# Last set of the retention's output projection by ordinary products, layer 2's input split over two sets, another form of the keys' norm, and retention tiles laid out anew

## The chip, the cores and the metric

The kernel runs on one core of a Trainium2 chip. A core has five engines with queues of their own, which meet only at semaphores: TensorE (PE, with its weight loads shown apart as PEld), VectorE (DVE), ScalarE (ACT), GpSimd (POOL) and SyncE (SP, which here only issues DMAs). Each queue runs in order: an instruction that waits holds all that stand behind it. The metric is the device time of one launch in microseconds (us), lower is better.

## The reference

One inference step of a two-layer decoder trunk over 1024 prompt tokens and 8 sample tokens, model width 1024, all in float32. Layer 1 is a retention, layer 2 attention in a sliding window:

```python
def retention_layer(x, S0, g_norm, w_in, g_out, w_out):      # 4 heads, DK 256, DV 512, chunks of 128
    h = rmsnorm(x, g_norm)
    q, k, v, gate = jnp.split(h @ w_in, [RET_QK, 2 * RET_QK, 2 * RET_QK + RET_V], axis=-1)
    k = k * (RET_DK ** -0.5)
    # chunk by chunk: o = (q k^T * decay) v + decay' * q S ;  S = S * decay'' + (k * decay''')^T v
    o, S = retention_scan(q, k, v, S0)
    o = rmsnorm(o, g_out) * jax.nn.silu(gate)                # 1024 x 2048
    return x + o @ w_out, S                                  # w_out is 2048 x 1024

def swa_layer(x, g_norm, w_in, q_gain, k_gain, sinks, w_out, ...):   # 16 heads, 2 key heads of 64
    h = rmsnorm(x, g_norm)
    q, k, v, gate = jnp.split(h @ w_in, [SWA_Q, SWA_Q + SWA_KV, SWA_Q + 2 * SWA_KV], axis=-1)
    q = rmsnorm(q, q_gain); k = rmsnorm(k, k_gain)           # per head of 64
    o = banded_attention(q, k, v, sinks) * jax.nn.silu(gate)
    return x + o @ w_out, k, v
```

The two row norms matter here. With x the row of layer 2's input (already times the gain), r = (mean(x^2) + EPS)^-0.5 and y = x @ w_k, a key is (r y) * (mean((r y)^2) + EPS)^-0.5 times its gain. Since r is one number per row, the same value is y * (mean(y^2) + EPS * (mean(x^2) + EPS))^-0.5.

## The kernel before, in words

A float32 operand of a product is split in a high half (rounded by ACT) and a low half (what is left, by a subtraction on DVE or POOL), and a product is three matmuls: high by high, low by high, high by low.

**Retention.** After the input projection (up to about 541 us) come 32 steps, one for each head and chunk, to about 684 us. A step (lines L778 to L1089) reads evp, evx and evc or evw, which SP loads from scratch tensors in DRAM, transposes them, makes S (the state's update) and po (the output) on PE, and on the side vh, vl, Sh, Sl (halves of the values and the state), the statistics ss and the normed output `on`, which PE transposes into `tr` at L104. All these tiles are cut out of one pool by `lay` in a written order, over the space of tiles that older work used; a tile must wait for the last reader of what lay there. The first two steps read operands that lie elsewhere (`first` in the profile). `x_decode` is a generator that loads the sample rows' input (memset on POOL, four DMAs on SP at L1117, transposes on DVE) in three parts, at steps of the table `others`.

**Output projection.** `psets` holds eight sets. Set n computes for half P = n // 4 of the inner width the quarter a = n % 4 of the output columns, 256 of them. A plain set has 8 slots of 24 matmuls (`p_plain`, L1301): 4 groups of tokens (keys c, w, x, p) by 2 halves t. The other kind has 14 slots of 12 matmuls (`p_prod`, L334 to L336): seven products of sums of quarters in the manner of Strassen and Winograd, for which POOL and DVE form the sums (`p_sum`: S1 to S4), ACT and DVE or POOL the halves (`p_hi`, `p_lo` at L1174), and for which the products are put together from PSUM banks that several results share (`p_evac`, L1196 to L1206). Sets 0 to 3 are plain and leave partial results in DRAM (`p_store`), which the sets 4 to 7 load (`p_part`) and add. `p_fins` then finishes a group of tokens: the gain and halves into SA, layer 2's input (L1251 on ACT, L1261 on DVE), its sum of squares `acc` (L1263), the columns for the sample rows, and a store of the residual.

SA also holds the operands B and T of the sets themselves, in cells that `CELL` numbers. So layer 2's input cannot be written in place where a cell is still read: the columns of sets 4 to 6 are stored to DRAM (`xscr`), loaded again (`a_load(k)`, 512 KB, k = 0 to 5, on SP) and split there (`a_split(k, 0)` on ACT, `a_split(k, 1)` on DVE at L1393); those of set 7 are written directly.

Between the slots of PE, the orders of ACT, DVE, POOL and SP are written by `later(slot, ...)` and `when(time, ...)`: the instruction goes into its engine's queue at that slot of PE's order.

**Layer 2's keys and values.** Nine chunks c = 0 to 8 (the last is the 8 sample rows). `kv_mm(c, h)` makes half h of a chunk's 24 matmuls (L1757 to L1759) into a bank that is `pj` or `sc` by turns. `rstd9` sums acc on PE and makes r9 and e9 = EPS * (mean + EPS) for four or five chunks; `kv_ev(c)` makes the values vv (ACT) and the normed key kd (ACT squares `kj`, DVE `kss`, POOL `krk`, DVE L1739); `kv_tr` transposes kd, and `kv_kk` splits it. Two chunks' first halves run ahead of the loop. Between them ACT and POOL convert weights for the next stage (`wh`, `wl`), and `rbcast_mm` spreads r9 into `rbc`. From about 908 us projections of q and gate run with the attention, whose order the scheduler of the language makes, and then the output projection.

## Time and profile before

| | us |
|---|---|
| median of 3 runs | 1314.88 (1314.08 to 1314.96) |
| the profiled execution | 1315.55 |
| its span, first to last instruction | 1313.6 |
| input projection, from the start to about | 541 |
| 32 steps of the retention, to about | 684 |
| sets 0 to 3, plain, to | 777.8 |
| sets 4 to 7, by seven products, to | 864.3 |
| keys and values, to | 908.4 |
| projections, attention, output, to the end | 1313.6 |

A row of a timeline gives start and duration in us, engine, line, operation and tiles, and in brackets how long the engine had been idle and what released it. Of the kinds of rows, the waits (engine and line that waited, what released it, us in total, times, longest) tell where an engine stood still; a table of windows gives for each stretch the busy time of each engine with its count of instructions, the clock that TensorE was granted, the busy share of the DMA engines and GB/s. A clock below 1.00 means that matmuls came at longer intervals in part of the window.

### The profile page before, as it was taken

The numbers are of one execution on the slowest core, as the hardware profiler recorded it, in microseconds if no ns is written. First come the engines' busy times: TensorE is split into PE (matmuls) and PEld (weight loads), VectorE is DVE, ScalarE is ACT, GpSimd is POOL, SyncE is SP. The second block draws the span as 40 slices with busy tenths as digits, with TensorE's granted clock in tenths as the row PEclk, the third lists the DMA queues.
The fourth block names the chain that finished last, engine by engine and source line by source line (L and its number), as shares of the span: only waits on it lengthen the run. The fifth ranks groups of instructions, "written<-read, shape, count | busy, mean of one in ns | idle before, by whom it ended". The sixth has DMA issues, their size and how long they took to land.

```text
span 1313.6 us, 26814 instructions
## 1 busy us (share of the span) xinstructions
PE 1271.3 (97%) x9815; PEld 1217.2 (93%) x9815; DVE 764.5 (58%) x1475; ACT 668.7 (51%) x1656; POOL 754.3 (57%) x903
## 2 busy tenths in 40 slices
PE   6999999999999999899999999978999999999998
PEld 6999999999999999888889999968998999998998
DVE  6944556565566674477763755653665666766321
ACT  5533544554555553578761343445576676666121
POOL 6654544545458898789661658626476676554000
PEclk9999999999999999999999999999998999999999
DMA  6314767677676754556879856732032211237232
GB/s 225 104 60 129 239 197 243 182 234 220 197 221 188 231 179 121 173 170 205 270 208 280 210 178 173 209 88 85 17 98 81 65 57 42 77 108 252 73 96 77
DMA packets 220911, 205.62 MB, mean 157 GB/s; under 512 B 32697, under 2 KB 195765, under 8 KB 220765
## 3 DMA queue, kind: packets, MB, share of 16 engines
q1 hardware_dynamic: 188784, 169.56, 43.1%
q10 hardware_dynamic: 31996, 34.36, 8.2%
q8 instruction: 77, 1.26, 0.4%
q14 instruction: 54, 0.43, 0.1%
HBM read 134.36 MB, written 70.55 MB: 156 GB/s over the span
## 4 chain that ended last, share of the span: by engine, by line
PE 84%; POOL 5%; DVE 3%; ACT 3%; issue 2%; DMA 2%; SPq 0%; ACTq 0%; POOLq 0%; DVEq 0%
PE S L1301 7%; PE b L334 7%; PE b L336 7%; PE b L335 7%; PE pj L1654 6%; PE pj L1655 6%; PE pj L1656 6%; PE b L327 4%; PE tr L104 4%; PE b L328 4%; PE b L329 4%; PE o L2017 2%; PE b L543 2%; PE sc L1980 1%; PE S L336 1%
## 5 line engine op out<-in xcount | busy, mean ns | idle before, releaser
L334 PE MATMUL b<-xh,woh 128*128 128x258 f32 x784 | 223.2, 285 | 0.0
L336 PE MATMUL b<-xh,wol 128*128 128x258 f32 x784 | 221.9, 283 | 1.3 <-POOL wol L225 1.3
L335 PE MATMUL b<-xl,woh 128*128 128x258 f32 x784 | 221.6, 283 | 0.0
L1654 PE MATMUL pj<-SA,wh 128*128 128x384 f32 (+1 forms) x512 | 174.8, 341 | 2.1 <-ACT SA L2037 1.3
L1655 PE MATMUL pj<-SA,wh 128*128 128x384 f32 (+1 forms) x512 | 164.7, 322 | 0.2 <-DVE SA L2038 0.2
L1656 PE MATMUL pj<-SA,wl 128*128 128x384 f32 (+1 forms) x512 | 164.8, 322 | 0.0
L334 PEld LDWEIGHTS b<-xh,woh 128*128 128x128 f32 x784 | 148.0, 189 | 4.1 <-issue 4.1
L336 PEld LDWEIGHTS b<-xh,wol 128*128 128x128 f32 x784 | 148.0, 189 | 1.7 <-POOL wol L225 1.7
L335 PEld LDWEIGHTS b<-xl,woh 128*128 128x128 f32 x784 | 148.7, 190 | 0.0
L225 POOL TENSOR_TENSOR wol<-raw,woh 128x512 fp32r<-128x512 f32 x52 | 68.1, 1319 | 119.7 <-ACT woh L220 108.6
L327 PE MATMUL b<-woh,xh 128*128 128x256 f32 x448 | 126.6, 283 | 0.0
L328 PE MATMUL b<-wol,xh 128*128 128x256 f32 x448 | 126.0, 281 | 0.0
L329 PE MATMUL b<-woh,xl 128*128 128x256 f32 x448 | 125.6, 280 | 0.0
L1654 PEld LDWEIGHTS pj<-SA,wh 128*128 128x128 f32 x512 | 97.0, 190 | 5.9 <-issue 2.6
L1655 PEld LDWEIGHTS pj<-SA,wh 128*128 128x128 f32 x512 | 97.3, 190 | 0.4 <-DVE SA L2038 0.4
L1656 PEld LDWEIGHTS pj<-SA,wl 128*128 128x128 f32 x512 | 96.7, 189 | 0.0
L1995 POOL TENSOR_TENSOR s<-s,sm 128x512 f32<-128x512 f32 x64 | 66.6, 1040 | 47.9 <-DVE sm L1994 43.7
L327 PEld LDWEIGHTS b<-woh,xh 128*128 128x128 f32 x448 | 84.3, 188 | 5.0 <-issue 2.9
L220 ACT ACTIVATE woh<-s 128x512 fp32r<-128x512 f32 x88 | 54.1, 624 | 59.7 <-POOL s L210 22.0
L329 PEld LDWEIGHTS b<-woh,xl 128*128 128x128 f32 x448 | 84.3, 188 | 0.0
L328 PEld LDWEIGHTS b<-wol,xh 128*128 128x128 f32 x448 | 84.3, 188 | 0.0
L1987 ACT ACTIVATE s<-s,mx 128x257 f32<-128x257 f32 x128 | 64.2, 505 | 36.1 <-DVE mx L1985 35.3
(521 smaller groups left out, 3650.4 us busy)
## 6 DMA issues: line engine op xcount, KB each, us to landing
raw<-in_w_in_ret_dram ACTq DMA_DIRECT2D x44, 512.0 KB
st<-in_state_ret_dram SPq DMA_DIRECT2D x64, 256.0 KB
out_dram<-st SPq DMA_DIRECT2D x64, 256.0 KB
vb<-vscr SPq DMA_DIRECT2D x64, 128.0 KB
evp<-qks SPq DMA_DIRECT2D x32, 256.0 KB
evx<-vsc SPq DMA_DIRECT2D x32, 256.0 KB
wr<-in_w_in_swa_dram SPq DMA_DIRECT2D x32, 256.0 KB
evc<-gsc SPq DMA_DIRECT2D x16, 256.0 KB
```

Of the source, the lines that this page charges most:

```text
L225: eng.tensor_tensor(lo, src_of(s, name, sub), hi.bitcast(F32), SUB)
L327: mm(dst, xh, wh, start=a and i == 0, stop=False, skip_group_check=True)
L328: mm(dst, xh, wl, start=False, stop=False, skip_group_check=True)
L329: mm(dst, xl, wh, start=False, stop=z, skip_group_check=True)
L334: mm(dst, wh, xh, start=a, stop=False, **sg)
L335: mm(dst, wh, xl, start=False, stop=False, **sg)
L336: mm(dst, wl, xh, start=False, stop=z, **sg)
L1301: mm(box[0], s.op[f"A{i + 1}{j + 1}", 0][w][:, k, :], xs_[t][x[j]][:, k, :], start=(xs_ is XH and w == 0 and j + k == 0), stop=(xs_ is XL ...
L1654: mm(ps, hi[:, k, fs], xh[:, k, t0:t1], start=first and k == ks[0], stop=False)
L1655: mm(ps, hi[:, k, fs], xl[:, k, t0:t1], start=False, stop=False)
L1656: mm(ps, lo[:, k, fs], xh[:, k, t0:t1], start=False, stop=last and k == ks[-1])
L1995: nc.gpsimd.tensor_tensor(st[:, :, 0:256], st[:, :, 0:256], sm.unsqueeze(2).broadcast_to([128, 2, 256]), ALU.mult)
```

## The change

Seven things are done at once.

1. Set 7 becomes a plain set: 192 matmuls in place of 168, without S1 to S4, with four operands instead of seven to split, and with its own banks for every result. `p_part` loads all four partial tiles of it into ring tiles, and `p_plain`, for a set with P = 1, finishes each group of tokens by `p_fins` after slot 3 of the set at the earliest.
2. In the sets that are not plain, the low half of A22 goes from POOL to DVE (`p_lo`).
3. The cells of B and T are numbered anew, so that cells 0 to 3 hold T2 and T1. `a_load` of k = 0 to 3 goes to slots 4 to 7 of set 6 (v is its first slot, u that of set 7), with splits at v+9, v+12, u and u+2; k = 4 and 5 are loaded at u+4 and split at u+5 and u+6.
4. Set 7 reads T3 as its plain operand: it is loaded again from DRAM at slots v+10 and v+11 and split at u and u+1. So that it is still there, the sums that were stored over it go to a scratch of their own, `tsc`.
5. `knorm_a` adds e9 in place of EPS and takes the squares without the scale r; the product of krk with r falls away; vv stands behind the squares in ACT's order. Both forms give the same key, as shown above.
6. No first half of a chunk runs ahead: `kv_mm(n, 0)` stands right in front of `kv_mm(n, 1)` and what belongs between them.
7. `x_decode` has its parts at steps 2, 5 and 9 in place of 3 and 6; the tiles of the retention lie in another order, with a smaller pad.

The first place is SP's order in the retention, where the sample rows' input is loaded (`ra`). Before:

```order
L734 DMA evp<-qks 128x512 x2
L741 DMA evx<-vsc 128x512
L747 DMA evc<-gsc 128x512
L734 DMA evp<-qks 128x512
L741 DMA evx<-vsc 128x512
L747 DMA evw<-gsc 128x512
L1117 DMA ra<-in_x_sample_dram 8x4x64 x4
```

After:

```order
L742 DMA evx<-vsc 128x512
L748 DMA evc<-gsc 128x512
L735 DMA evp<-qks 128x512
L742 DMA evx<-vsc 128x512
L748 DMA evw<-gsc 128x512
L1119 DMA ra<-in_x_sample_dram 8x4x64 x4
```

The four DMAs stand two steps' loads (six rows) later; the step's own three loads follow behind them in both.

The second place is DVE's order in set 7 of the output projection. L1393 is `a_split`, L1261 and L1263 finish columns, L1203 and L1200 empty banks of the seven products. Before:

```order
L1200 TENSOR_TENSOR evx<-b_11089,evp 128x258
L1393 SCALAR_TENSOR_TENSOR SA<-SA,gcol 128x1024
L1200 TENSOR_TENSOR evx<-b_11106,evp 128x258
L1393 SCALAR_TENSOR_TENSOR SA<-SA,gcol 128x1024
L1174 TENSOR_TENSOR w_9196<-s2b,w_9196 128x512
L1203 TENSOR_TENSOR evc<-S,evc 128x258
L1393 SCALAR_TENSOR_TENSOR SA<-SA,gcol 128x1024
L1261 SCALAR_TENSOR_TENSOR SA<-evc,gcol,SA 128x2x128
L1203 TENSOR_TENSOR evc<-S,evc 128x258
L1393 SCALAR_TENSOR_TENSOR SA<-SA,gcol 128x1024
L1261 SCALAR_TENSOR_TENSOR SA<-evc,gcol,SA 128x2x128
```

After, where L1308 empties a bank of a plain set and L1341 splits T3:

```order
L1308 TENSOR_TENSOR evc<-S,evc 128x258
L1341 TENSOR_TENSOR SB<-SB 128x2x256
L1396 SCALAR_TENSOR_TENSOR SA<-SA,gcol 128x1024
L1308 TENSOR_TENSOR evc<-S,evc 128x258
L1341 TENSOR_TENSOR SB<-SB 128x2x256
L1308 TENSOR_TENSOR evp<-S,evp 128x258
L1396 SCALAR_TENSOR_TENSOR SA<-SA,gcol 128x1024
L1308 TENSOR_TENSOR evp<-S,evp 128x258
L1262 SCALAR_TENSOR_TENSOR SA<-evc,gcol,SA 128x2x128 x2
L1264 TENSOR_TENSOR acc<-acc,tr 128x4x128
```

Six splits stood in set 7; four are left there, and two stand among the bank emptyings of set 6.

The third place is ACT's order where the keys and values begin: vv (L1764, then L1770), the squares kj (L1730, then L1737), the weights wh and the spread r9, rbc. Before:

```order
L1764 ACTIVATE vv<-pj,r_78 128x128
L1730 ACTIVATE kj,kss<-pj,r_78 128x64 x2
L1626 ACTIVATE wh<-wr 128x512
L1822 ACTIVATE rbc<-pm 128x384
L1764 ACTIVATE vv<-sc,r_78 128x128
```

After:

```order
L1737 ACTIVATE kj,kss<-pj 128x64 x2
L1770 ACTIVATE vv<-pj,r_79 128x128
L1633 ACTIVATE wh<-wr 128x512
L1827 ACTIVATE rbc<-pm 128x384
L1737 ACTIVATE kj,kss<-sc 128x64 x2
```

The squares come first and read no r; wh and rbc of the first chunks stand where they stood, ahead of chunk 1.

The diff, cut to its core:

```diff
-    for n_, x_ in enumerate((B11, T2, T1, B21, T3, B22, T4)):
+    for n_, x_ in enumerate((T2, T1, B11, B21, T3, B22, T4)):
...
-    lay("Sh1", "Sl1", "sT0", "sTh0", "sTl0", "on0", "qh0", "ql0", "kh0", "kl0", "sT1", "ss0", "ss1", "vl0",
-        "on1", "vh1", "vl1", "kh1", "kl1", "pad", "Sh0", "Sl0", "vh0", "qh1", "ql1", "sTh1", "sTl1")
+    lay("Sh1", "Sl1", "sT0", "sTh0", "sTl0", "qh0", "ql0", "kh0", "kl0", "ss0", "ss1", "sT1", "on1", "kh1", "kl1",
+        "pad", "on0", "vh0", "vl0", "sTh1", "sTl1", "qh1", "Sh0", "Sl0", "vh1", "vl1", "ql1")
...
-        s.n, s.P, s.a, s.kind, s.fw, s.plain = n, n // 4, n % 4, "p", 128, n < 4
+        s.n, s.P, s.a, s.kind, s.fw, s.plain = n, n // 4, n % 4, "p", 128, n < 4 or n == 7
...
-        eng = eng or (pool if name in ("A12", "A22") else dve)
+        eng = eng or (pool if name == "A12" or (name == "A22" and s.plain) else dve)
...
-        if key in "cw":
+        if key in "cw" or s.plain:
             t = c_tile(s, key)
...
-        if t:
+        if s.P:
+            p_fins(s, key, t, max(n, s.n0 + 3))
+        elif t:
             later(n + 2, p_store, s, key)
...
-            nc.sync.dma_start(out=osc[0, 1, t][:, ks], in_=z)
+            nc.sync.dma_start(out=tsc[t][:, ks], in_=z)
...
-        for k in range(6):
-            later(u + 1 + k, a_load, k)
-            later(u + 4 + k, a_split, k, 0)
-            later(u + 5 + k, a_split, k, 1)
+        for t in range(2):
+            later(v + 10 + t, o_load, raw_of(T3, t)[:, :, 0:256], 0, 1, t)
+            split(u + t, T3, t)
+        DC(u + 1, T3, True)
+        for k, (a, b) in enumerate(((v + 4, v + 9), (v + 5, v + 12), (v + 6, u), (v + 7, u + 2), (u + 4, u + 5), (u + 4, u + 6))):
+            later(a, a_load, k)
+            later(b, a_split, k, 0)
+            later(b + 1, a_split, k, 1)
...
-        if i in (3, 6):
-            next(xdg)
+        if i in (2, 5, 9):
+            next(xdg, None)
...
-            nc.scalar.activation(kj[:n], src[:, g * 64:g * 64 + 64], AF.Square, scale=r, accum_out=ss[:n, g:g + 1])
-        nc.vector.tensor_scalar(ss[:n], ss[:n], 1.0 / HD, EPS, ALU.mult, ALU.add)
+            nc.scalar.activation(kj[:n], src[:, g * 64:g * 64 + 64], AF.Square, accum_out=ss[:n, g:g + 1])
+        nc.vector.tensor_scalar(ss[:n], ss[:n], 1.0 / HD, e, ALU.mult, ALU.add)
...
-        nc.gpsimd.tensor_scalar(rk[:n], rk[:n], r, None, ALU.mult)
...
-        nc.scalar.activation(vv[:, c, :], ps[:, 128:256], AF.Copy, scale=r)
-        rk = knorm_a(ps[:, 0:128], r, 128)
+        rk = knorm_a(ps[:, 0:128], e9[:, c:c + 1], 128)
+        nc.scalar.activation(vv[:, c, :], ps[:, 128:256], AF.Copy, scale=r9[:, c:c + 1])
...
-    kv_mm(0, 0)
-    kv_mm(1, 0)
     for n in range(9):
-        if n < 7:
-            kv_mm(n + 2, 0)
+        kv_mm(n, 0)
```

## The prediction

> **What bounds the kernel now.** I read the page first, then the list of what TensorE waited for, then tables of windows, and last the rows around each wait.

> ```profile
> span 1313.6 us, 26814 instructions
> PE 1271.3 (97%) x9815; PEld 1217.2 (93%) x9815; DVE 764.5 (58%) x1475; ACT 668.7 (51%) x1656; POOL 754.3 (57%) x903
> PE 84%; POOL 5%; DVE 3%; ACT 3%; issue 2%; DMA 2%; SPq 0%; ACTq 0%; POOLq 0%; DVEq 0%
> PE pj L1757 <- DVE kd L1739: 3.3, 1, 3.3
> PE S L334 <- DVE evw L1203: 2.4, 2, 2.3
> PE pj L1757 <- DVE evx L1203: 2.3, 1, 2.3
> PE sc L1757 <- ACT wh L1626: 2.3, 1, 2.3
> PE S L336 <- POOL w L1174: 2.0, 2, 1.3
> PE pj L1654 <- ACT wh L1626: 0.8, 1, 0.8
> PE sc L1757 <- DVE evp L1203: 0.6, 1, 0.6
> PE tr L104 <- DVE kkl L1784: 0.6, 1, 0.6
> ```

> TensorE (PE) is busy 97% of the span and carries 84% of the chain that ended last. So another engine's work costs something only where PE stands still for it, and a removed matmul is worth its issue interval. In the list (us, times, longest) the waits at L334 and L336 belong to the output projection of the retention, those at L1757 to the keys and values of layer 2. The windows of these stages (busy us of PE, PEld, DVE, ACT, POOL; clock; DMA share; GB/s) say where PE stands:

> ```profile
> 820.00:841.00 21.00, 21.00 (x177) 21.00 (x176) 13.71 (x24) 9.17 (x21) 17.65 (x13) 1.00 0.59 163
> 841.00:864.30 23.30, 20.88 (x170) 20.29 (x168) 19.04 (x25) 13.52 (x22) 10.02 (x6) 1.00 0.57 180
> 864.30:884.00 19.70, 13.48 (x101) 13.06 (x100) 8.03 (x27) 4.85 (x14) 3.77 (x6) 0.91 0.40 112
> 884.00:908.40 24.40, 20.50 (x146) 18.91 (x146) 8.68 (x33) 13.68 (x51) 14.64 (x21) 0.93 0.16 45
> ```

> Set 6 (first row) leaves PE no gap; set 7 leaves 2.4 us; the stage of keys and values (last two rows, 44.1 us) leaves 44.1 - 13.48 - 20.50 = 10.1 us, and its clock is below 1. That stage is the largest pocket of idle TensorE that the edits touch.

> **The change, part by part.**

> *Start of the retention.* The tiles Sl0, vh0 and vl0 lie elsewhere.

> ```profile
> 543.73 0.39 PE L1022 MATMUL po<-first 128*128 128x512 f32 x1
> 547.13 0.66 PE L104 MATMUL tr<-ident,on 128*128 128x128 f32 x4 [3.01 <-DVE on L1066]
> 544.22 1.29 DVE L1048 SCALAR_TENSOR_TENSOR Sl<-S,Sh 128x512 fp32r<-128x512 f32 x2 [5.28 <-PE po L1022]
> 544.16 0.63 ACT L810 ACTIVATE vh<-evx 128x512 fp32r<-128x512 f32 x1 [1.66 <-PE po L1022]
> ```

> The second step's last matmul (543.73) is what both DVE's Sl (L1048, idle 5.28 before it) and ACT's vh (idle 1.66) wait for, since these tiles lie on operands of that step. Behind Sl in DVE's order stands `on`, for which PE then waits 3.01. In the new layout the vector engine's wait on that matmul is gone: Sl needs only ACT's Sh, and vh waits for no matmul. `on` still needs po, some statistics on ACT and POOL's power; I leave 0.3 of the 3.01 and take **-2.7** (bounds -3.0 and -1.5: the first if all of the wait goes, the second if only ACT's 1.66 goes).

> *Sample row's load.* Its memset goes from step 3 to 2, its four DMAs from 3 to 5, its transposes from 6 to 9.

> ```profile
> 558.89 3.01 SPq L1117 DMA_DIRECT2D ra<-in_x_sample_dram  x4
> 566.02 0.63 ACT L810 ACTIVATE vh<-evx 128x512 fp32r<-128x512 f32 x1 [2.84 <-DMA evx<-vsc]
> 567.63 0.68 PE L778 MATMUL tr<-evp 128*128 128x128 f32 x4 [1.51 <-issue]
> ```

> SP's queue stood before these DMAs for POOL's memset, then took 3.01 us to issue them; evx behind them came late, ACT waited 2.84 and PE 1.51. Two steps later SP meets a finished memset. The 3.01 us of issue stay and push the loads of one step; without the wait for the memset I expect the steps' lead to cover them: **-1.5** (bounds -1.5 and 0: the stall may only move two steps).

> *A22's low half from POOL to DVE in sets 4 to 6.*

> ```profile
> 796.83 0.39 PE L336 MATMUL S<-SB,w 128*128 128x258 f32 x1 [1.31 <-POOL w L1174]
> 793.79 1.74 POOL L1206 TENSOR_TENSOR evx<-evx,rx 128x516 f32<-128x516 f32 x1
> 795.49 1.28 POOL L1174 TENSOR_TENSOR w<-ra,w 128x512 fp32r<-128x512 f32 x1
> 851.50 1.79 DVE L1174 TENSOR_TENSOR w<-s2b,w 128x512 fp32r<-128x512 f32 x1
> ```

> PE waits for a subtraction that stands on POOL behind a 1.74 us sum and takes 1.28 itself. The 2.0 us of the list are two such waits, in sets 4 and 5; set 6 has none. The same line on DVE has taken 1.79 at its longest (last row), and DVE, busy 13.7 of 21 us, reaches it earlier. I take **-2.0** (bounds -2.2, with the slower first matmul after each stall, and -0.7, if only the shorter wait goes).

> *Set 7 by ordinary products.* 192 matmuls in place of 168.

> ```profile
> L1301 PE MATMUL S<-SA,EO x48: 277/282/368, 684.5 to 690.6; 128*128 128x258 f32 x48
> L1301 PE MATMUL S<-SB,w x288: 278/283/290, 719.8 to 777.7; 128*128 128x258 f32 x144
> 860.75 0.36 PE L334 MATMUL S<-SB,w 128*128 128x258 f32 x1 [2.25 <-DVE evw L1203]
> 858.17 1.50 DVE L1261 SCALAR_TENSOR_TENSOR SA<-evc,gcol,SA 128x256 fp32r<-128x256 f32 x1
> 856.18 2.07 DVE L1393 SCALAR_TENSOR_TENSOR SA<-SA,gcol 128x1024 fp32r<-128x1024 f32 x1
> 860.53 1.27 DVE L1393 SCALAR_TENSOR_TENSOR SA<-SA,gcol 128x1024 fp32r<-128x1024 f32 x1
> ```

> The 32 slots of sets 0 to 3 (these rows are the first and last group) run from 684.5 to 777.8 with 0.7 us of transposes between: 92.6 / 32 = 2.9 us a slot. Set 7 becomes 8 x 2.9 = 23.2 us, against 23.3 now: the 24 added matmuls (2.9) eat the removed waits (2.4) and their ramps. The 2.25 us wait goes because DVE no longer runs six splits (L1393) and the chain over one shared bank in the same slots: I count 4 splits x 1.27, 8 evacuations x 0.42, 8 x 0.5 and 4 x 0.7 of finishing and four of 0.7, 18 of 23.2 us, with the evacuations spread over all 8 slots. POOL loses its sums. **-0.1** (bounds -2.4, if tails of the old set are longer than I see, and +2.9, if a DVE stall of the same size comes back).

> *Input split over two sets.* Four of the six 512 KB loads, two of the splits and two reloads of T3 (512 KB each) go to set 6 or its end. That hides under PE's 21 us if DVE and the DMA engines keep up: DVE 13.7 + at most 1.8 (A22) + 2 splits of 1.27 to 2.07 = at most 19.6 of 21; DMA 163 + 3.1 MB / 21 us = 311 GB/s, while the present set 7 moved this while it loaded the same columns:

> ```profile
> 846.00:851.00 5.00, 5.00 (x43) 5.00 (x43) 3.65 (x7) 2.82 (x3) 0.79 (x2) 1.00 0.93 326
> ```

> So set 6 is filled nearly to what one stretch has shown; the leads are 4 to 9 slots of 1.43 us. I cost it at **0**; without cover it is the third rival. The split's own duration is 1.27 at 860.53, when POOL is idle, and 2.07 at 856.18, when POOL runs. [...]

> *Keys and values.* Three edits act together.

> ```profile
> 866.60 0.55 PE L1757 MATMUL pj<-kv,SA 128*128 128x256 f32 x1 [2.29 <-DVE evx L1203]
> 869.09 0.41 PE L1759 MATMUL pj<-kv,SA 128*128 128x256 f32 x1
> 871.65 0.28 PE L1757 MATMUL pj<-kv,SA 128*128 128x256 f32 x1
> 875.78 0.28 PE L1759 MATMUL sc<-kv,SA 128*128 128x256 f32 x1
> 881.66 0.36 PE L1757 MATMUL pj<-kv,SA 128*128 128x256 f32 x1 [3.29 <-DVE kd L1739]
> 880.91 0.61 DVE L1739 SCALAR_TENSOR_TENSOR kd<-pj,krk,kgb 128x128 f32<-128x128 f32 x2 [1.22 <-POOL krk L1737]
> 875.01 0.43 SPq L1692 DMA_DIRECT2D kgb<-in_k_norm_dram  x1
> ```

> (1) The first wait, 2.29, and the 0.6 behind it are for DVE, 7 us late at the end of set 7, to empty banks and finish columns; after a plain set only the last slot is open, some 2 us of work (0.42, ACT 0.5, 0.5, 0.7) against the first chunk's 1.4 us on columns that are ready: both waits go. (2) Two chunks' first halves no longer run ahead, so chunk 0 is complete after 2.8 us and its sum of squares starts there, no longer needing r, and the multiply by r on POOL is gone. PE now needs kd of chunk 0 after four chunks of 24 x 0.118 = 2.8 us (36 matmuls from 871.65 to 875.78) less a half, and the norms' small products, about 11.4 us after set 7. kd's own chain: the row sums stand on PE 4.3 after set 7, DVE's e and POOL's two powers take some 3 more (an estimate from kd's 880.91 less the sums at 875.90, the multiplies left out), and then kgb must have landed. kgb is issued 10.7 us after set 7's end now, behind the weight loads on SP; with DVE some 5 us earlier I estimate its landing at 9 to 10. So the 3.3 goes, and with it the 2.3 behind ACT's wh (ACT had stood before it for rbc and chunk 1's squares at once). Of the 10.1 us I keep the last two waits, 0.6 and 0.8, and 0.3 more: -8.4. (3) The twelve matmuls from 866.60 to 869.09 come every 0.226 us, not 0.118: 1.3 us lost; a second such stretch, near 890, I estimate from the 0.93 of that window at 1.3 more. With no gap ahead of them both go: -2.6. Together **-11.0** (bounds -12.7, everything, and -5, the first two waits and their slow stretch).

> [...]

> **Sum.** 1315.55 (the profiled execution; its span is 1313.6) - 2.7 - 1.5 - 2.0 - 0.1 - 0 - 11.0 = 1298.25. The median of the runs shown, 1314.88, is 0.67 lower, so **1297.6** by it. After 908 I let the weight conversions of the attention part stand as they are.

> **The rivals.**

> A. *Keys' stage stays bound by its chain.* SP issues weights, constants and kgb in order behind the sample's stores, ACT's wh of chunk 0 waits for the weights and chunk 1's squares wait behind it and rbc. Without the two chunks ahead, PE has less to run meanwhile. Then only the first two waits and their stretch go: -5, so 1303.6 (1302 to 1307). For it: kgb's late issue; against it: DVE's and the last store's earlier end.

> B. *The moves in the retention do nothing:* a tile in its new place waits for another old owner, and the loads' issue makes the same gap at step 5. 1297.6 + 4.2 = 1301.8. For it: 3.01 us of issue stay; against: Sl has no wait on a matmul left.

> C. *Slower.* Set 6's loads land after the slot in which their split stands in DVE's order. DVE then waits for a DMA with evacuations and low halves queued behind it, and PE waits for these: per split what 860.75 shows, 2.25. Six splits make 13.5; with 2.9 for the added matmuls, the 2.4 saved, the keys' stage beginning with as late a DVE as now (no gain there) and the 6.2 of the retention and A22: +13.5 + 2.9 - 2.4 - 6.2 = +7.8, 1322.7. It decides once loads take over 5.7 us (four slots). For it: 311 GB/s and up to 19.6 of 21 us; against: 326 GB/s with PE dense at 846 to 851.

> **How the numbers follow.** Forecast 0.66 (1291.5 to 1301.5), A 0.18, B 0.09, C 0.07. The range 1291.5 to 1307.5 holds the forecast's bounds, A and B; outside lie C and edges. About 0.2% (2.6 us) can be told from no change: faster 0.92 (all but C, with a crumb off A), same 0.03, slower 0.05.

> **What would show it.** Right: no wait above 1 us of PE at `on` near 547 and at the low half of A22; set 7 near 23.2 us without waits; the next stage 32 to 34 us with clock near 1.0. Wrong: kd or wh again 2 us ahead of L1757's successor (A); 1 us or more of waiting in sets 6 and 7 released by a DMA or a split (C); the attention part longer by over 2 us, of which my sum says nothing.

## The result and the profile after

The changed kernel takes 1295.19 us (median of 4 runs, 1293.7 to 1295.33) against 1314.92 us before (median of 4, 1314.08 to 1315.85) on the same chip: a ratio of 0.9847, 95% interval 0.983 to 0.9864. That is 19.7 us less; 1297.6 was forecast, with a range of 1291.5 to 1307.5. The profiled execution after took 1293.7 us, its span is 1291.9.

What TensorE waited for after (list of waits; engine, line and what released it, us in total, times, longest), from the retention to the start of the keys' stage, in that stage, and behind it. Lines have moved by 1 to 7: L105 was L104, L779 was L778, L1763 was L1757.

```profile
PE tr L105 <- DVE on L1067: 0.7, 2, 0.5
PE tr L779 <- DMA evp<-qks: 0.3, 1, 0.3
PE S L335 <- DVE evp L1204: 0.2, 1, 0.2
PE tr L105 <- DVE kkl L1789: 1.2, 1, 1.2
PE pm L1894 <- ACT sq L1873: 2.9, 1, 2.9
PE pj L1661 <- ACT SA L2042: 1.3, 1, 1.3
```

None of the waits at L1757, L334 and L336 that the prediction quoted is left. The first two rows are the retention: 3.5 us have become 0.7, and the 1.5 at `issue` is gone. The 1.2 us for `kkl` stand 10 us behind the start of the query products, where there was no wait before; the 0.6 that the old list had for `kkl` were inside the keys' stage, and are gone. The wait of 2.9 at the squares `sq`, in the attention, was 2.7 before.

The windows of sets 6 and 7 and of the keys' stage after (busy us of PE, PEld, DVE, ACT, POOL; clock; DMA share; GB/s):

```profile
814.00:835.00 21.00, 20.83 (x173) 20.65 (x173) 15.68 (x26) 10.31 (x23) 16.55 (x11) 1.00 0.96 293
835.10:858.30 23.20, 23.20 (x194) 23.20 (x193) 19.32 (x29) 14.46 (x27) 5.36 (x4) 1.00 0.51 153
858.30:888.00 29.70, 29.70 (x247) 29.03 (x246) 13.42 (x53) 14.26 (x58) 16.43 (x20) 1.00 0.40 111
```

TensorE is busy through all of set 7 and all of the keys' stage, at full clock. Set 7 takes 23.2 us and the keys 29.7, where they took 23.3 and 44.1. Set 6 moved 293 GB/s at a DMA share of 0.96, and TensorE lost 0.17 us in it.

The start of the retention after (a timeline; start, duration, engine, line, operation, and in brackets the idle time before it and what ended it):

```profile
543.78 0.39 PE L1023 MATMUL po<-first 128*128 128x512 f32 x1
544.36 0.66 PE L105 MATMUL tr<-ident,on 128*128 128x128 f32 x4 [0.19 <-DVE on L1067]
540.86 1.29 DVE L1049 SCALAR_TENSOR_TENSOR Sl<-S,Sh 128x512 fp32r<-128x512 f32 x2 [1.87 <-ACT Sh L1037]
543.55 0.75 DVE L1067 TENSOR_SCALAR on<-po,ss 128x512 f32<-128x512 f32 x1 [0.93 <-POOL ss L120]
```

Sl ran 2.9 us before the step's last matmul instead of behind it, so `on` stood ready.

To place the 21.7 us between the two spans I take, from the timelines, the start of the first matmul of each part: the retention's steps, set 0, set 4, the first product of the keys, the first of the queries. This gives the time of each part, for both kernels and for all that were run after them (us; the ratio is to the kernel before, on the same chip and with its interval):

| kernel | retention | sets 0 to 3 | sets 4 to 7 | keys | from the queries on | median | ratio |
|---|---|---|---|---|---|---|---|
| before | 145.4 | 93.4 | 88.8 | 41.8 | 405.2 | 1314.92 | |
| changed | 141.7 | 93.4 | 84.2 | 29.7 | 403.9 | 1295.19 | 0.9847 (0.983 to 0.9864) |
| a_same | 141.8 | 94.5 | 84.3 | 29.7 | 405.8 | 1294.21 | 0.9845 (0.9825 to 0.9865) |
| u_order | 142.5 | 93.9 | 84.0 | 36.2 | 404.8 | 1301.23 | 0.9891 (0.9874 to 0.9909) |
| u_norm | 141.2 | 93.4 | 83.8 | 30.2 | 404.7 | 1293.41 | 0.9832 (0.9814 to 0.985) |
| u_kvboth | 141.8 | 94.0 | 83.8 | 39.9 | 404.5 | 1302.71 | 0.9903 (0.9888 to 0.9919) |
| o_one | 141.6 | 93.4 | 84.3 | 30.4 | 405.4 | 1295.39 | 0.9851 (0.9829 to 0.9873) |
| u_set7 | 141.4 | 93.4 | 86.3 | 31.0 | 406.2 | 1298.01 | 0.9856 (0.9838 to 0.9875) |
| u_lay | 145.2 | 93.9 | 84.1 | 29.7 | 406.4 | 1299.17 | 0.9865 (0.9843 to 0.9886) |
| u_xdec | 142.9 | 93.4 | 84.4 | 29.7 | 406.5 | 1295.86 | 0.9844 (0.9824 to 0.9863) |
| u_a22 | 141.1 | 93.4 | 86.8 | 29.7 | 404.6 | 1297.64 | 0.9861 (0.9833 to 0.9889) |
| x_load2 | 141.9 | 93.5 | 92.8 | 29.7 | 407.8 | 1305.44 | 0.992 (0.9896 to 0.9943) |
| v_lo | 141.3 | 93.4 | 83.8 | 29.7 | 403.2 | 1293.96 | 0.9837 (0.9815 to 0.9859) |
| v_both | 141.9 | 93.4 | 84.0 | 29.7 | 406.1 | 1294.35 | 0.984 (0.9822 to 0.9858) |

One of the four runs of x_load2 took 1532.75 us at a mean clock of 0.754, and its row leaves that run out.

From before to changed: retention -3.7, sets 4 to 7 up to the first product of the keys -4.6, keys -12.1, the rest -1.3. The wait of 2.3 us ahead of the first product of the keys counts in the third column of numbers. The intervals are some 0.4% wide, so by time alone only the undone order (u_order, u_kvboth) and x_load2 stand clear of the changed kernel; for the smaller effects I go by the parts and the waits inside them. The retention's column varies by up to 1.4 us among kernels with the same retention, the last one by up to 4.6 with hardly any edit in it.

### The profile page after: what moved, and what is told of

It is laid out like the page before. It is cut to its first block, busy times and chain, and to the rows that moved or that the text cites. A ratio compares the mean times of both kernels' runs of the same rounds, so it can differ in the third digit from the quotient of the medians.

```text
span 1291.9 us, 26845 instructions
## 1 busy us (share of the span) xinstructions
PE 1266.7 (98%) x9839; PEld 1214.1 (94%) x9839; DVE 767.1 (59%) x1473; ACT 666.8 (52%) x1656; POOL 742.4 (57%) x887
## 3 DMA queue, kind: packets, MB, share of 16 engines
q1 hardware_dynamic: 189840, 170.61, 44.1%
q8 instruction: 78, 1.28, 0.4%
## 4 chain that ended last, share of the span: by engine, by line
PE 85%; POOL 5%; DMA 4%; DVE 2%; ACT 2%; issue 2%; SPq 0%; ACTq 0%; POOLq 0%; DVEq 0%
PE S L1302 9%; PE b L335 7%; PE b L337 7%; PE b L336 7%; PE pj L1661 6%; PE pj L1662 6%; PE pj L1663 6%; PE b L328 4%; PE b L329 4%; PE b L330 4%; PE tr L105 4%; PE o L2022 2%; PE b L544 2%; PE sc L1985 1%; PE S L1017 1%
## 5 line engine op out<-in xcount | busy, mean ns | idle before, releaser
L336 PE MATMUL b<-xl,woh 128*128 128x258 f32 x784 | 221.6, 283 | 0.0
L1661 PE MATMUL pj<-SA,wh 128*128 128x384 f32 (+1 forms) x512 | 174.4, 341 | 1.3 <-ACT SA L2042 1.3
L336 PEld LDWEIGHTS b<-xl,woh 128*128 128x128 f32 x784 | 148.7, 190 | 0.0
L1661 PEld LDWEIGHTS pj<-SA,wh 128*128 128x128 f32 x512 | 96.7, 189 | 4.8 <-issue 2.6
L328 PEld LDWEIGHTS b<-woh,xh 128*128 128x128 f32 x448 | 84.3, 188 | 5.0 <-issue 2.9
L330 PEld LDWEIGHTS b<-woh,xl 128*128 128x128 f32 x448 | 84.3, 188 | 0.0
L329 PEld LDWEIGHTS b<-wol,xh 128*128 128x128 f32 x448 | 84.3, 188 | 0.0
```

Of the source, the lines that this page charges most:

```text
L328: mm(dst, xh, wh, start=a and i == 0, stop=False, skip_group_check=True)
L329: mm(dst, xh, wl, start=False, stop=False, skip_group_check=True)
L330: mm(dst, xl, wh, start=False, stop=z, skip_group_check=True)
L336: mm(dst, wh, xl, start=False, stop=False, **sg)
L1661: mm(ps, hi[:, k, fs], xh[:, k, t0:t1], start=first and k == ks[0], stop=False)
```

## The experiments

**The tiles of the retention (u_lay).** The old layout with its larger pad, all else as changed (cut):

```diff
-    lay(... "sT1", "on1", "kh1", "kl1", "pad", "on0", "vh0", "vl0", ..., "Sh0", "Sl0", "vh1", "vl1", "ql1")
+    lay(... "on0", ..., "vl0", "on1", "vh1", ..., "pad", "Sh0", "Sl0", "vh0", "qh1", "ql1", "sTh1", "sTl1")
```

> The changed kernel with the retention's tiles laid as before. If the place of Sl0, vh0 and vl0 made the wait near 547 us: TensorE waits about 3.0 us again for `on`, vector engine idle about 5.3 us before Sl, kernel +2.8 us. Rival (the wait went for another reason, for example the sample load's new place): no wait above 0.5, kernel +0.

Timeline of that kernel:

```profile
545.41 0.87 PE L105 MATMUL tr<-ident,on 128*128 128x128 f32 x3 [3.01 <-DVE on L1067]
542.51 1.29 DVE L1049 SCALAR_TENSOR_TENSOR Sl<-S,Sh 128x512 fp32r<-128x512 f32 x2 [5.26 <-PE po L1023]
```

Both numbers of before came back, 3.01 and 5.3, and with them 3.5 us of the retention's part. Not all of the 3.5 is the wait: in this run the granted clock also stood at half from 545.49 to 548.90, which it did not in the kernel before. The place of a tile, with no instruction added or moved, was worth the whole wait. The first reading holds.

**The sample rows' load (u_xdec).** The parts at steps 3 and 6 again, as in the diff of the change, read backwards.

> The changed kernel with the sample rows' load at steps 3 and 6 as before. My reading: SyncE waits for the memset and one step's values come late: TensorE waits about 1.5 us near 565, kernel +1.5 (with the drain of the pipe up to 1.9). Rival (the stall was covered or only due to the old layout): +0 to +0.4.

TensorE's timeline of that kernel:

```profile
564.53 0.68 PE L779 MATMUL tr<-evp 128*128 128x128 f32 x4 [1.48 <-issue]
```

The stall is back at its old size; the retention's part grew by 1.3, the kernel's time by less than it can tell. With the load at step 5 the four DMAs still took 3.01 us of SyncE, and the steps' lead covered them.

**A22's low half (u_a22).** On GpSimd in all sets:

```diff
-        eng = eng or (pool if name == "A12" or (name == "A22" and s.plain) else dve)
+        eng = eng or (pool if name in ("A12", "A22") else dve)
```

> The changed kernel with A22's low half on GpSimd in sets 4 to 6. My reading: waits of about 1.3 and 0.7 us in sets 4 and 5, sets 4 to 6 together 2.0 to 2.5 us longer, kernel +2.0 to +2.5. Rival (set 6, now full of loads and splits, gains most from the move or loses by it): a third wait in set 6, or 1 us less than in sets 4 and 5.

The row of its list of waits:

```profile
PE S L337 <- POOL w L1175: 2.5, 2, 1.3
```

Two waits again, and sets 4 to 7 took 2.6 us more. The rival did not show: set 6, though fuller, has no third one.

**Set 7 by seven products, and all loads and splits in it (u_set7).**

```diff
-    ... s.plain = ..., n < 4 or n == 7
+    ... s.plain = ..., n < 4
-    enumerate((T2, T1, B11, B21, T3, B22, T4))       # the cells, in both places
+    enumerate((B11, T2, T1, B21, T3, B22, T4))
-        (T3 loaded again and split; a_load and a_split over sets 6 and 7)
+        for k in range(6):
+            later(u + 1 + k, a_load, k)
+            later(u + 4 + k, a_split, k, 0)
+            later(u + 5 + k, a_split, k, 1)
```

> The changed kernel with set 7 by seven products again and all six loads and splits of layer 2's input in set 7, cells numbered as before; order and norm of the keys' stage, tiles, sample load and A22 stay changed. My reading: set 7 takes 23 us with its 2.4 us of waits; then VectorE is 7 us late with the last columns, which the first chunk's second half now needs 1.4 us into the stage: TensorE waits 5 to 6 us there: stage 35 to 38 us, kernel +6 to +9 us. Rival (only the first two waits, 2.3 and 0.6, come back): stage 32.5 to 33.5, kernel +3 to +4.

Its list of waits, and TensorE's timeline around the first of them:

```profile
PE S L335 <- DVE evw L1204: 2.1, 1, 2.1
PE pj L1759 <- DVE evx L1204: 1.2, 1, 1.2
PE tr L1675 <- DVE acc L1264: 0.3, 1, 0.3
```

```profile
853.84 0.45 PE L335 MATMUL S<-SB,w 128*128 128x258 f32 x1 [2.08 <-DVE evw L1204]
854.08 0.42 PE L336 MATMUL S<-SB,w 128*128 128x258 f32 x1
854.29 0.42 PE L337 MATMUL S<-SB,w 128*128 128x258 f32 x1
```

Set 7's own wait came back (2.1), with matmuls every 0.21 us behind it, at half clock until 857.36. But of the 5 to 6 us that I expected in the keys' stage came 1.2 ahead of it and 1.4 in it. The rival was nearer: sets 4 to 7 and the keys together 3.5 us longer. VectorE's backlog at the end of the old set 7 was real (its last columns were finished at 863.97 + 0.48, 6 us after the set's last matmul), yet the first chunk's second half did not wait for those columns.

**The order and the norm of the keys' stage (u_order, u_norm, u_kvboth).** The order:

```diff
+    kv_mm(0, 0)
+    kv_mm(1, 0)
     for n in range(9):
-        kv_mm(n, 0)
+        if n < 7:
+            kv_mm(n + 2, 0)
```

> The changed kernel with two chunks' first halves ahead again in the keys' stage; all else as changed. My reading (banks and the chain of chunk 0): chunk 4's first half then needs chunk 0's bank about 9.3 us after set 7, while its kd ended 11.0 us after it (it waits for kgb), so TensorE waits there 1.7 to 3 us and the row of stalls returns in part: stage 32 to 35 us in place of 29.65, kernel +2 to +5 us. Rival (a plain set 7 alone made the stage dense, the order is free): stage 29.5 to 30.2, kernel within 0.6 us of the changed one.

The norm:

```diff
-            nc.scalar.activation(kj[:n], src[...], AF.Square, accum_out=ss[:n, g:g + 1])
-        nc.vector.tensor_scalar(ss[:n], ss[:n], 1.0 / HD, e, ALU.mult, ALU.add)
+            nc.scalar.activation(kj[:n], src[...], AF.Square, scale=r, accum_out=ss[:n, g:g + 1])
+        nc.vector.tensor_scalar(ss[:n], ss[:n], 1.0 / HD, EPS, ALU.mult, ALU.add)
+        nc.gpsimd.tensor_scalar(rk[:n], rk[:n], r, None, ALU.mult)      # and vv ahead of the squares
```

> The changed kernel with the keys' norm as before (squares scaled by r, krk times r, vv first). My reading (the shorter chain is hidden: chunk 0's kd waits for kgb until 10.5 us after set 7 in either form): stage +0 to +0.8 us, kernel +0 to +1. Rival (the norm's chain carries the stage): each of eight chunks 0.3 to 0.6 longer, stage +2.5 to +5 us, with TensorE waiting for kd.

Both:

> The changed kernel with the order and the norm of the keys' stage both as before, so that of what acts on that stage only the plain set 7 with the split input is left. If plain set 7 is the cause (no backlog on VectorE, banks free): stage 31 to 34 us. If the order and the norm are the cause: stage 38 to 44 us, kernel +8 to +14. More than the two single runs together would mean that each covers for the other.

The order alone costs 6.6 us of the stage, more than either reading had it. Order and norm both undone (u_kvboth) cost 7.5 us of the kernel's median, a little under the 8 to 14 expected. Windows and rows of u_order:

```profile
857.50:869.50 12.00, 9.70 (x83) 9.49 (x81) 4.74 (x20) 2.64 (x9) 2.92 (x5) 0.98 0.57 151
869.50:875.00 5.50, 5.40 (x31) 5.12 (x32) 0.52 (x4) 0.63 (x3) 1.57 (x3) 0.72 0.00 0
875.00:878.80 3.80, 2.30 (x20) 2.13 (x19) 1.66 (x5) 2.46 (x11) 3.37 (x5) 1.00 0.00 0
```

```profile
869.60 0.55 PE L1763 MATMUL pj<-kv,SA 128*128 128x256 f32 x1 [2.40 <-DVE kd L1745]
877.25 0.36 PE L1763 MATMUL sc<-kv,SA 128*128 128x256 f32 x1 [1.50 <-DVE kd L1745]
863.56 0.23 ACT L1737 ACTIVATE kj<-pj 128x64 f32<-128x64 f32 x1 [4.17 <-PE pj L1765]
874.37 0.49 ACT L1827 ACTIVATE rbc<-pm 128x384 f32<-128x384 f32 x1 [6.28 <-PE pm L1826]
```

With two halves ahead, chunk 0 was complete only 5.9 us into the stage (ACT's first square at 863.56; in the changed kernel, whose stage starts at 858.34, it is 861.45, 3.1 us in). Its key was done at 869.46, and TensorE stood until 869.60 for the bank that it frees, chunk 4's. Counted from the start of the stage, chunk 4 asked for that bank at 9.6 us and the key was done at 11.9; in the changed kernel the key is done at 11.2, TensorE transposes it at 12.6, and chunk 4 needs the bank only at 14.2. So most of the change is that the bank is asked for earlier, and only 0.7 us that the key is later. The stall also held what stands behind on TensorE: the product pm, for which ACT's rbc waited 6.28 us, with the squares of chunk 1 behind it, whose key then made the second wait. Added up: waits 2.4 + 1.5 + 0.5 (ahead of the first query product), and 0.72 of the clock over 5.5 us (1.5 us) make 5.9; the other 0.7 stands around the three waits, some 0.24 us each, where the list does not count it.

The norm is hidden under the changed order (+0.5 us of the stage, as expected), since chunk 0's key waits for its gain there in either form (it starts 4.24 us behind the issue of kgb's load in the changed kernel, and 4.25 in u_norm):

```profile
868.88 0.61 DVE L1745 SCALAR_TENSOR_TENSOR kd<-pj,krk,kgb 128x128 f32<-128x128 f32 x2 [2.96 <-DMA kgb<-in_k_norm_dram]
864.64 0.43 SPq L1699 DMA_DIRECT2D kgb<-in_k_norm_dram  x1
```

(rows of the changed kernel). Under the old order it is not hidden: 39.9 - 36.2 = 3.7 us, of which 1.7 are longer waits and 1.9 are clock, since TensorE ran at half clock for 6.8 us of that stage and for 3.4 in u_order. Both undone cost 10.3 of the stage, where the single runs add up to 7.1; each covers for part of the other, but most of that difference is the clock of one execution each, and the medians of u_order and u_kvboth do not tell the two apart. Neither order and norm nor plain set 7 are the sole cause: the old order and norm on top of a plain set 7 make 39.9 us, the new order and norm on top of the old set 7 make 31.0, against 41.8 with all old and 29.7 with all new. Order and norm are the larger part.

**One chunk ahead (o_one).** Between none and two:

```diff
+    kv_mm(0, 0)
     for n in range(9):
-        kv_mm(n, 0)
+        if n < 8:
+            kv_mm(n + 1, 0)
```

> The changed kernel with one chunk's first half ahead in the keys' stage, between the changed order (none) and the one before (two). If the stalls come when a PSUM bank is asked for before its key is done: chunk 0's key is then done some 10.4 us after set 7 and chunk 4 asks for its bank at 11.2, chunk 1's is done at 15.5 and asked for at 15.4: stage 29.7 to 30.5 us. If each chunk ahead costs by itself, by delaying all later steps: half of 6.6 us, stage 32.5 to 33.5 us.

30.4 us, 0.7 more than with none, not half of 6.6. Chunk 4 asked for its bank 12.6 us into the stage, and chunk 0's key was done at 11.1, so nothing waited there. So the cost is not in proportion to what runs ahead: it comes when a bank is asked for before the key that frees it is done.

**Set 6's loads twice (x_load2).**

```diff
             later(a, a_load, k)
+            if k < 4:
+                later(a, a_load, k)
```

> The changed kernel with the four 512 KB loads of k = 0 to 3 in set 6 issued twice, one after the other to the same place (2.1 MB more in about 20 us, on a stretch that already shows a DMA share of 0.96). If set 6 is on the edge (rival C of the prediction): the splits stand late in VectorE's and ScalarE's orders, TensorE waits 2 us or more in set 6 or 7, kernel +3 to +10. If the leads of 5 to 9 slots have room: no wait above 0.5 us, kernel within 0.6 us.

SyncE's waits, and one row each of ACT and TensorE:

```profile
SPq L1388 <- DMA SA<-xscr: 19.3, 4, 6.6
848.84 1.15 ACT L1339 ACTIVATE SB<-SB 128x512 fp32r<-128x512 f32 x2 [10.85 <-DMA SB<-osc]
852.23 1.01 PE L1302 MATMUL S<-SB,w 128*128 128x258 f32 x3 [7.29 <-ACT SB L976]
```

TensorE waited 7.3 us, ran at half clock until 855.44 (clock 0.77 from 850 to 862), and sets 4 to 7 took 8.6 more. But this run did not press the DMA engines, as I had meant it to: the second load of a tile waits on SyncE for the first to land (19.3 us in four waits), and the reload of T3, which is set 7's operand, stood behind in that queue. So it says where the change is thin: T3's reload, through SyncE's order. It does not say what more bytes would do. What the changed kernel shows of those is the window of set 6 above, and within it

```profile
824.00:829.00 5.00, 5.00 (x44) 5.00 (x43) 3.59 (x7) 2.61 (x6) 4.62 (x3) 1.00 1.03 384
```

five microseconds at 384 GB/s with TensorE dense.

**Two tries to go on (v_lo, v_both), and the changed kernel again (a_same).** The largest waits left in the later part are the 2.9 us at `sq`, 1.3 at L1661, which was there before, and the 1.2 at `kkl`. Two of them were tried.

```diff
-                lo_eng[0].tensor_tensor(lo[:, js, :], raw[...], hi..., ALU.subtract)
+                e_ = nc.vector if (j, i) in dv else lo_eng[0]      # dv: (1, 0), (1, 2) of the query weights at p = 4
+                e_.tensor_tensor(lo[:, js, :], raw[...], hi..., ALU.subtract)
```

> The changed kernel with two of the low halves of weights (second half of the query weights of heads 8 to 11) formed on VectorE and not on GpSimd. The wait of 2.9 us at the squares near 974 hangs on ACT's `oh`, which waits for GpSimd's `ot` behind such a low half of 1.28 us: the wait falls to 1.3 to 1.7 us, and less time is lost to the clock behind it: kernel -1 to -2.5 us. Rival (ACT is then late by its own waits for the weights' loads): the wait stays within 0.4 of 2.9, kernel -0.4 to +0.4.

```diff
     until(RQ, (0, 0))
+    fill(ps, 2.0)
     pt = dec_cache(0)
```

> As the kernel before it, and two more us of projection matmuls stand ahead of the first transposes of the cached keys, for which TensorE waits 1.2 us in the changed kernel (ACT's high half of a key block stands behind weights that are still being loaded). Expected: that wait goes too, kernel another -0.5 to -1.4 us. Rival (the work put there is only taken from a later gap's cover): same as the kernel before it within 0.4 us, with a new wait later.

> The changed kernel once more, beside the next three on one chip: 1295 us within 1.5, the stage of keys and values 29.65 us again, the part behind it between 403.9 and 406.5 us, since that part varied over the profiled executions by a clock that one or two windows lose.

Waits of v_lo (first row) and of v_both:

```profile
PE pm L1895 <- ACT sq L1874: 2.1, 1, 2.1
```

```profile
PE pm L1895 <- ACT sq L1874: 2.2, 1, 2.2
PE sc L1986 <- DVE s L1989: 0.9, 1, 0.9
```

The first wait fell to 2.1, by 0.8 and not by 1.2 to 1.6: ACT's `oh` still waits 1.4 us for GpSimd's `ot`, which starts at 967.25, while ACT itself is still copying its inputs (966.66 to 967.44). In v_both the wait for `kkl` is gone, and 0.9 us stand at a new place. The medians, 1293.96 and 1294.35 against 1294.21 for the same changed kernel beside them, tell no difference, and neither of the gains expected is shown. So no version is shown to beat the changed one. a_same itself came as expected in time and in the keys' stage; its last part is within the range, while its sets 0 to 3 took 94.5 us, 1.1 more than the same code in the run before, with only 0.2 us of waits listed there. Of the 1.1 us 1.0 lies at six starts of TensorE, between 703.0 and 704.7 and near 733.5, which came 0.19 to 0.51 us apart in place of 0.12; what slowed them is open.

## Why the prediction was right, point by point

**The bound and the direction.** TensorE carried the time, and its idle pockets went away one by one. Each of the four cheap terms came out near its size:

- *Start of the retention:* forecast -2.7; the wait went from 3.01 to 0.19, and came back whole with the old layout.
- *Sample rows' load:* forecast -1.5; the 1.5 went, and came back with the old steps.
- *A22:* forecast -2.0 with bounds -2.2 and -0.7; undone it costs 2.6 (waits of 2.5). A little outside the bound, since set 5's wait was longer there.
- *Set 7:* forecast 23.2 us without waits; it is 23.2 without waits. The forecast cost of the split input, 0, held: set 6 lost 0.17 us, at 293 GB/s (311 forecast) and VectorE busy 15.7 of 21 us (at most 19.6 forecast, with splits of 1.27 to 2.07 us; all six took 1.27 or 1.28).

**Keys and values: the mechanism right, the size too small.** Forecast -11.0 with a bound of -12.7. From the end of set 7 (864.15) the stage took 44.25 us and now takes 29.65: -14.6, beyond the bound. The 14.6 are 10.1 us of listed waits, 3.0 of half clock and 1.5 around the waits. Three terms of the forecast were mis-sized. I kept 1.7 us of waits, of which none is in the stage now. I summed the listed idle time as if it were all that a wait costs; but around the wait of 3.29 TensorE's starts lie 3.56 us apart (878.10, the last product before it, and 881.66), and the next 0.20, where 0.118 each would do: 3.52 lost for 3.29 listed. The seven waits make 1.5 us of that kind. And the slow stretches, 2.6 in my sum, were 3.0: half clock from 866.25 to 869.66 and from 890.14 to 893.55, in which TensorE had work for 6.0 us.

**The credit within that stage.** Step (1) of the prediction put the first two waits and their slow stretch, 2.29 + 0.6 + 1.3 = 4.2 us, down to VectorE's backlog behind the old set 7. u_kvboth has the plain set 7 under the old order and norm: neither wait is there, and the stage, from the end of set 7, is 39.94 us, 4.3 less than before. So the step holds under the old order. Under the new one the same backlog costs less: u_set7 lost 1.2 us ahead of the stage and 1.4 in it. (The bound of -5 "for the first two waits and their slow stretch", and with it the price of rival A, is 4.2 by these terms.)

Step (2), order and norm, was right in its times: it had chunk 0 complete after 2.8 us (3.1 measured), its key needed 11.4 us after set 7 (12.6) and kgb landed at 9 to 10 (10.5, from the start of the key). Its size was too small: with the second slow stretch it carries 6.8 of the 11.0, and measured it is 39.94 - 29.65 = 10.3. The order alone makes 6.6 of it. The norm, which the step names beside it, is worth 0.5 us in the changed kernel, because the key waits for kgb there in either form.

**The part behind.** Its -1.3 us were not in the sum, and are not shown to be the change's: the same kernel gave 403.9 and 405.8. The granted clock alone can make such a difference: it stood at half for 10.2 us of that part before, for 3.4 in the changed kernel and for 6.8 in a_same. New with the change is the wait of 1.2 for `kkl` there. ACT's high half of a key block stands behind weights (wait of 2.3 us for wr); that these have less time to arrive since the stage is shorter is likely, but not tested. So a small part of the gain is given back.

**The sum.** -3.7, -4.6, -12.1 and -1.3 by parts against a forecast of -17.3 in all: right in each cheap term, 3.6 too little in the keys, and the median 2.4 below the number. The parts add up to 21.7, 2 us more than the medians differ by, since the profiled execution before (1315.55) lay above its median and the one after (1293.7) below.

**The rivals.** A (the keys' chain): no wait of TensorE in that stage, though kgb landed later than forecast; under the old order TensorE did wait for keys (2.4 and 1.5 us in u_order). B (the retention's moves do nothing): refuted by u_lay and u_xdec. C (loads that are late for their splits): did not occur; x_load2 shows that its mechanism exists, by SyncE's order and T3 rather than by the input's splits, and that held-up loads can cost 8.6 us.

```profile
850.54:853.95 3.41, 1.33 (x12) 1.15 (x11) 3.41 (x7) 2.40 (x5) 0.00 (x0) 1.00 0.13 38
853.95:857.36 3.41, 3.41 (x17) 3.41 (x18) 3.41 (x6) 2.45 (x5) 0.00 (x0) 0.50 0.26 77
867.17:870.58 3.41, 1.08 (x9) 1.11 (x10) 0.78 (x3) 0.67 (x3) 2.25 (x3) 1.00 0.00 0
870.58:874.00 3.42, 3.42 (x18) 3.07 (x17) 0.52 (x4) 0.00 (x0) 0.35 (x1) 0.50 0.00 0
876.49:879.90 3.41, 1.89 (x16) 1.68 (x15) 1.18 (x6) 1.48 (x6) 1.15 (x2) 1.00 0.29 81
879.90:883.32 3.42, 1.66 (x15) 1.69 (x15) 0.61 (x2) 0.11 (x1) 2.11 (x3) 1.00 0.02 5
883.32:886.73 3.41, 3.16 (x25) 2.65 (x23) 0.62 (x5) 1.58 (x7) 1.55 (x2) 1.00 0.00 0
```

A wait of 2.08 us (u_set7) lay inside one step, and the next step ran at half clock. Of a wait of 3.29 us in u_kvboth 2.3 lay in one step:

```profile
869.50 0.36 PE L1764 MATMUL pj<-kv,SA 128*128 128x256 f32 x1 [3.29 <-DVE kd L1746]
```

Matmuls came at full rate directly behind it, and at half clock from 870.58 on, 1.08 us later. The wait of 3.29 us in the kernel before fell on two steps, with 1.52 and 1.76 us idle, and the clock stayed at 1.00. In the 14 traces, from the start of each one's clock record at 14 to 17 us, each of the 20 steps with 1.8 us or more of idle TensorE was followed by one at half clock; of those with 1.2 to 1.8 us, 6 of 48 were (3 of 3 and 0 of 9 in the kernel before, 1 of 1 and 0 of 3 in the changed one). So in these traces the half clock goes with the idle time that falls into one step, and not with the length of the wait. The second half of a stretch of 6.83 us is not told by this count: in the kernel before, the step from 992.54 on had 0.87 us idle, and the next was at half clock as well. That the slow stretches of the keys' stage would go with the gaps ahead of them was my estimate; the clock of 1.00 from 858.30 to 888.00 in the changed kernel shows them gone, and the 2.6 us that I took by the rows were near the 3.0 measured.

## What to carry to other kernels

Running work ahead on the bounding engine is not free cover: where banks are few, it delays the first consumer and asks for its bank earlier (here two chunks ahead cost 6.6 us of the stage, one 0.7), so compare when a bank is asked for with when it is freed before you add or drop a prefetch. Price a stall on TensorE by the distance of the starts around it and not by the listed idle time alone (0.2 us more a wait here), and add the half clock that may follow, here 3.41 or 6.83 us of it. A wait with no data behind it, such as an engine that waits for a matmul of an older step, may be only the address of a tile; moving the tile can be worth as much as moving work (here the wait of 3.01 us).

## What the runs showed that I had not expected

By where it fell on the grid of the clock, the same wait cost half clock or none: behind 3.29 us came half clock from 870.58 on in u_kvboth, and none in the kernel before. The wait of 2.08 us in u_set7 so cost some 1.5 us more (about 16 matmuls at 0.21 in place of 0.118). Even without a wait the clock can drop: in the kernel before, with TensorE busy throughout,

```profile
1248.40:1268.40 20.00, 20.00 (x128) 19.28 (x127) 2.98 (x8) 2.57 (x9) 0.00 (x0) 0.91 0.32 98
```

and in the changed one the same stretch of work ran at full clock:

```profile
1228.00:1248.00 20.00, 20.00 (x140) 19.28 (x139) 3.03 (x8) 3.01 (x9) 0.00 (x0) 1.00 0.35 101
```

The loss is a single step of that grid, and in the step ahead of it stands a row of 16 narrow matmuls (kernel before):

```profile
1256.64 1.96 PE L2117 MATMUL o<-pm,wr 128*128 128x16 f32 x16
1255.37:1258.78 3.41, 3.41 (x28) 3.04 (x26) 0.56 (x1) 0.14 (x1) 0.00 (x0) 1.00 0.00 0
1258.78:1262.19 3.41, 3.41 (x13) 3.41 (x12) 0.65 (x3) 1.11 (x5) 0.00 (x0) 0.50 0.69 219
```

These matmuls have 16 columns each, start 0.11 us apart for 1.81 us, and count as busy in full. In the five traces in which the row lies wholly inside one step (before, u_lay, u_xdec, x_load2 and v_both) the next step is at half clock; in the nine in which the end of a step divides it (at 1237.75 in the changed kernel, with the row from 1236.62 on), none is. Whether the row is the cause was not tested. So some 1.7 us (half of 3.41) are lost in one execution and not in another at the same stretch of work, most of a 0.2% effect.
